# A hybrid diffusion step on one Trainium2 core: more begun strips, two places for a row, two-bank scores, and strips moved into the latents

## The chip, the core and the metric

The kernel runs on one core of one Trainium2 chip. Five engines matter: PE (TensorE, matmuls, with PEld, its weight loads), DVE (VectorE), ACT (ScalarE), POOL (GpSimd) and SP (SyncE, which only issues transfers). The metric is the time of one execution on the device in microseconds; before the change its median over 3 runs is 3182.38 us (3175.32 to 3186.39).

## The reference, cut to what matters

One inference step through two trunk layers, for 128 context tokens and 512 latent ones, 1024 wide. Each layer is half a SwiGLU, a mixer, half a SwiGLU, each behind an RMSNorm with shift, scale and gate from the conditioning.

```python
def swiglu(x, w_gu, w_down):
    g, u = jnp.split(x @ w_gu, 2, axis=-1)
    return (jax.nn.silu(g) * u) @ w_down

def pre(x, g, m, j):
    return rmsnorm(x, g) * (1.0 + m[:, :, 3 * j + 1]) + m[:, :, 3 * j]

# layer 0: p + mu * (0.5 * (prev + next) - p), and conv3(p, w)
# layer 1: latent attention and a long convolution (Hyena), side by side
    s = jnp.einsum('bqhd,bkhd->bhqk', qn, k_nope) + jnp.einsum('bqhr,bkr->bhqk', qp, k_pe)
    prob = jax.nn.softmax(s.astype(jnp.float32) * scale, axis=-1)
    for n, gate in enumerate((x1, x2)):
        z = gate * (bidir_fftconv(z, h[:, n, 0], h[:, n, 1]) + bias[n] * z)
```

`w_gu` is 1024 x 5632, `w_down` 2816 x 1024. Layer 0's mixer projects onto 32 strips of 128 columns (15 for RWKV-7, each shifted as in the comment; 17 for the gated delta rule, 12 of them convolved over three tokens). Layer 1's projects onto 6 strips for the latents of attention (8 heads) and 12 for Hyena.

## The kernel before

All activations lie as [channel, token], in two halves `c` of 320 tokens. Each float32 operand of a large product is split into a rounded part and a rest (`wh`, `wl`, `hh`, `hl`), and a product is three matmuls per 128 channels. The split is a cast on ACT and a subtraction on DVE (L469 to L471, L654, L655). A "strip" is a product with 128 columns of a weight: one load of 512 KB on SP, one cast, one subtraction, 48 matmuls of 320 columns (`strip`, L773).

**A feed-forward block** (`ffn`, L632) has 22 strips of the hidden width in five groups (`FGROUPS`), and after each group a down-projection over 8 column blocks `d`. The 2 x 2 blocks of a strip's gate and up weights against two token halves take seven half products of 12 matmuls (`strip`, L680): the two that need the first half's tokens alone give `u` and `s`, and five need sums and differences of the tokens' quarters (`b`, `hidh`, `hl`, made in `quarters`, L591) and of the weights (`S`, on POOL, L684). The quarters need the norm of the second token half, which comes last out of the branch before. To bridge that, the first `NE` = 5 strips are *begun*: `first` (L666) loads a strip's first weights, makes the two early half products, 24 matmuls, and keeps them in `u2` and `s1` until the strip itself runs, with 60 matmuls then instead of 84. The strip loads the same weights a second time. The four blocks are named by layer and place: 01, 02, 11, 12.

The shift, scale and gate (*modulation*) come from 16 chunks of a 1024 x 1024 product that run in the background of blocks 01 and 02, eight in each. A chunk is four items; an item is four loads of 256 KB into tiles `wmod` and 8 matmuls. `background(n)` (L315) uses n items at a call and `fetch` (L305) loads ahead, `(bufs + 1) // 4` items deep: two, with `NMOD` = 7 tiles. The call stands after each strip and each second `d` (L727, L737).

**Layer 0's input projection** (`in_proj0`, L838) writes each strip as a row `o` of 640 tokens to DRAM (`pd`). The shifted ones (`shift`, L873) sum two neighbours on POOL into `nb` and take one DVE pass; the convolved ones (`conv3`, L906) take two DVE passes. `t` (L275) keeps the first `bufs` with which a name is asked for in a pool; `shift` is called first, and asks for one.

**Layer 1's mixer** (`mixers1`, L2112) runs `latents` (L1635), then four heads of attention with three Hyena strips beside each (`hyena_in`, L1904), then Hyena's transforms (`hyena`, L1934) beside the other four, three parts at each head. A head has a projection and five blocks of 128 queries; a block (L1738) has scores in one or two PSUM banks, a maximum for each bank, an exponential for each with its sum, and joins of both; its weights are transposed on PE and copied to `PT` by DVE (L1779). The last head's output goes to DRAM (`mixd`) and comes back for the output projection.

The program is straight-line code. A scheduler orders each engine's instructions and inserts the waits; each engine, and SP's queue of loads, then runs strictly in that order.

## Time and profile before

| what | value |
|---|---|
| median of 3 runs | 3182.38 us (3175.32 to 3186.39) |
| the profiled execution, its time | 3187.08 us |
| the profiled execution, its span | 3185.1 us |
| granted PE clock, mean | 0.957 |
| block 01, 100 to 564 us: PE busy | 454.64 of 464 us |
| layer 0's mixer, 564 to 1265 us: PE busy | 623.86 of 701 us |
| blocks 02 and 11, 1340 to 2300 us: PE busy | 473.95 of 490 and 446.28 of 470 us |
| layer 1's mixer, 2300 to 2660 us: PE busy | 326.70 of 360 us |
| block 12, 2720 to 3185 us: PE busy | 438.23 of 465 us |

The profile is of one execution. A group row reads: source line, engine, operation, out<-in, shape, count | busy us, mean ns of one | idle us of the engine just before, and what ended it. PE's ends are modelled, so a busy PE is not always a PE at its peak. All matmuls stand on one line (L287), so they are told apart by their operands.

### The profile page before, as it was taken

What the parts mean: (1) busy time and instruction counts of PE and PEld (TensorE: products, weight loads), DVE (VectorE), ACT (ScalarE), POOL (GpSimd) and SP (SyncE); (2) the same over time, 40 slices, a digit from 0 to 9 for tenths busy, and PEclk for the clock granted to TensorE, in tenths of its full rate; (3) what the DMA queues carried; (4) which work ended last, traced back from release to release, by engine and by line L of the source; (5) the groups of instructions that cost most, each with busy time, mean ns of one, the idle gap of its engine ahead of it and who ended that gap; (6) DMA issues with size and microseconds to landing.
All of it is one profiled execution on the core that took longest, in us unless ns stands there. A gap on an engine that the chain in (4) does not pass through costs nothing.

```text
span 3185.1 us, 56006 instructions
## 1 busy us (share of the span) xinstructions
PE 2958.5 (93%) x21505; PEld 2671.5 (84%) x21505; DVE 2267.1 (71%) x4011; ACT 1355.0 (43%) x2846; POOL 1200.8 (38%) x1114
## 2 busy tenths in 40 slices
PE   7799999998988998889999979999989989899998
PEld 2689999987865676879999979999979748899998
DVE  5956667668769666695666797777766786977777
ACT  3423334566365555442333453333545424433333
POOL 1733335225545220263333474444310021744442
PEclk9999999998888989889999989999999989999999
DMA  7465542455564332445553222222321215222222
GB/s 273 137 209 164 177 137 72 166 157 170 139 151 112 93 86 81 161 146 181 163 180 116 82 93 87 84 86 83 122 62 58 91 47 181 67 90 86 80 83 83
DMA packets 277587, 385.36 MB, mean 121 GB/s; under 512 B 128704, under 2 KB 161120, under 8 KB 275400
## 3 DMA queue, kind: packets, MB, share of 16 engines
q1 hardware_dynamic: 277160, 381.13, 38.3%
q8 instruction: 169, 2.77, 0.4%
q14 instruction: 98, 0.80, 0.1%
q0 software_dynamic: 160, 0.66, 0.0%
HBM read 330.29 MB, written 51.42 MB: 120 GB/s over the span
## 4 chain that ended last, share of the span: by engine, by line
PE 54%; DVE 10%; ACT 4%; DMA 4%; POOL 3%; issue 3%; SPq 1%; DVEq 0%; ACTq 0%; POOLq 0%
PE ps L287 52%; DMA wr<-in_wd_dram 2%; DVE wl L655 1%; POOL S L684 1%; DMA wr<-in_wo_dram 1%; DVE nx L539 1%; DVE wl L471 1%; POOL X L826 0%; POOL wl L655 0%; POOL inv L824 0%; PE ps L1778 0%; DMA pd<-o 0%; DVE nacc L514 0%; DVE b L605 0%; ACT wh L470 0%
## 5 line engine op out<-in xcount | busy, mean ns | idle before, releaser
L287 PE MATMUL ps<-hh,wh 128*128 128x320 f32 x2208 | 698.6, 318 | 17.8 <-DVE g L1901 7.1
L287 PE MATMUL ps<-hl,wh 128*128 128x320 f32 x2208 | 695.1, 316 | 5.4 <-POOL hl L546 2.7
L287 PE MATMUL ps<-hh,wl 128*128 128x320 f32 x2208 | 686.5, 315 | 5.3 <-DVE wl L471 4.2
L287 PE MATMUL ps<-b,wh 128*128 128x320 f32 x2112 | 480.5, 315 | 32.5 <-DVE b L605 17.2
L287 PEld LDWEIGHTS ps<-hh,wh 128*128 128x128 f32 x2208 | 422.4, 192 | 34.4 <-DVE g L1901 7.9
L287 PEld LDWEIGHTS ps<-hl,wh 128*128 128x128 f32 x2208 | 422.8, 192 | 9.7 <-POOL hl L546 3.9
L287 PEld LDWEIGHTS ps<-hh,wl 128*128 128x128 f32 x2208 | 420.3, 191 | 8.8 <-DVE wl L471 5.4
L287 PEld LDWEIGHTS ps<-b,wh 128*128 128x128 f32 x2112 | 360.7, 192 | 40.5 <-DVE b L605 19.4
L287 PE MATMUL ps<-hidl,wh 128*128 128x320 f32 x1248 | 383.7, 309 | 0.0
L287 PE MATMUL ps<-hidh,wh 128*128 128x320 f32 x1248 | 383.2, 312 | 0.0
L287 PE MATMUL ps<-hidh,wl 128*128 128x320 f32 x1248 | 381.7, 309 | 1.0 <-DVE wl L471 1.0
L550 DVE SCALAR_TENSOR_TENSOR x<-ps,mod,x 128x128 f32<-128x128 f32 (+2 forms) x528 | 212.4, 435 | 212.3 <-PE ps L287 211.7
L655 POOL TENSOR_TENSOR wl<-S,wh 128x512 fp32r<-128x512 f32 x176 | 260.5, 1480 | 264.8 <-ACT wh L654 261.6
L684 POOL TENSOR_TENSOR S<-wr,wu 128x512 f32<-128x512 f32 x88 | 125.2, 1423 | 600.9 <-DMA wr<-in_wgu_dram 394.9
L287 PE MATMUL ps<-b,wl 128*128 128x320 f32 x1056 | 330.6, 315 | 9.4 <-DVE wl L655 6.1
L470 ACT CAST wh<-wr 128x512 fp32r<-128x512 f32 (+2 forms) x210 | 157.7, 754 | 407.0 <-PE ps L287 318.0
L654 ACT CAST wh<-S 128x512 fp32r<-128x512 f32 (+1 forms) x264 | 201.0, 763 | 216.0 <-PE ps L287 163.7
L471 DVE TENSOR_TENSOR wl<-wr,wh 128x512 fp32r<-128x512 f32 (+2 forms) x210 | 186.5, 891 | 82.9 <-ACT wh L470 80.9
L287 PEld LDWEIGHTS ps<-hidh,wh 128*128 128x128 f32 x1248 | 232.9, 188 | 13.3 <-issue 7.4
L287 PEld LDWEIGHTS ps<-hidh,wl 128*128 128x128 f32 x1248 | 233.4, 188 | 1.5 <-DVE wl L471 1.5
L287 PEld LDWEIGHTS ps<-hidl,wh 128*128 128x128 f32 x1248 | 234.1, 188 | 0.0
L287 PEld LDWEIGHTS ps<-b,wl 128*128 128x128 f32 x1056 | 202.3, 192 | 13.8 <-DVE wl L655 8.5
(457 smaller groups left out, 5971.2 us busy)
## 6 DMA issues: line engine op xcount, KB each, us to landing
wmod<-in_wmod_dram SPq DMA_DIRECT2D x288, 256.0 KB
wr<-in_wgu_dram SPq DMA_DIRECT2D x108, 512.0 KB
wu<-in_wgu_dram SPq DMA_DIRECT2D x88, 512.0 KB
wr<-in_wd_dram SPq DMA_DIRECT2D x80, 320.0 KB
wr<-in_wd_dram SPq DMA_DIRECT2D x96, 256.0 KB
pd<-o SPq DMA_DIRECT2D x32, 320.0 KB
wr<-in_abg_dram SPq DMA_DIRECT2D x17, 512.0 KB
wr<-in_wo_dram SPq DMA_DIRECT2D x16, 512.0 KB
```

Source lines behind the costliest of these rows:

```text
L287: self.nc.tensor.matmul(out=out, lhsT=lhsT, rhs=rhs, start=start, stop=stop)
L470: nc.scalar.copy(out=wh, in_=w)
L471: nc.vector.tensor_sub(out=wl, in0=w, in1=wh.bitcast(F32))
L539: nc.vector.scalar_tensor_tensor(out=xn[:, a:b], in0=self.x[c][:, k, a:b], scalar=A, in1=r[:, a:b], op0=ALU.mult, op1=ALU.mult)
L550: self.nc.vector.scalar_tensor_tensor(out=self.x[c][:, d, a:b], in0=q[:, a:b], scalar=gate[:, cond, d:d + 1], in1=self.x[c][:, d, a:b], op ...
L654: nc.scalar.copy(out=hi, in_=r)
L655: eng.tensor_tensor(out=lo, in0=r, in1=f32(hi), op=ALU.subtract)
L684: G.tensor_tensor(out=out, in0=x, in1=y, op=op)
```

## The change

Five things change.

1. **Begun strips.** `NE` becomes a triple: block 01 keeps 5; block 02, where the second half of the modulation still runs, begins 10; blocks 11 and 12, with no modulation left, begin 9. In block 02 the last six of the ten lie in shared tiles `ew`, and these six take the modulation's weights afterwards: the modulation opens after strip 7, `fetch` is one item deep (six tiles), and 2 items follow each of strips 8 to 16, none stand in the first group's down-projection.
2. **Rows `o`.** Both places are taken at the start, and `shift` uses `conv3` with the weights hmu, omu, hmu; `nb` and POOL's sum go.
3. **Scores.** Both key halves lie in one tile of two PSUM banks: one maximum, one exponential with its sum, no joins.
4. **Strips in the latents.** Three of the twelve Hyena strips run in `latents`: one after the query latents, two at its end. Three heads (`NHS`) take the other nine.
5. **Hyena beside five heads**, two parts at each, and for these heads the copies to `PT` are ACT's.

```diff
-NE = 5
+NE = (5, 10, 9)
...
+NHS = 3
...
+        late = bool(self.bg) and w == 2
+        early, ne = {}, NE[1 if late else 2 if not self.bg else 0]
+        n0 = NE[0] - 1 if late else ne
+        shared = lambda: self.t(fp, [P, 2, H], "ew", bufs=ne - n0)
...
+            if f < n0:
+                p1, s1 = tile("u2", n0), tile("s1", n0 + 1)
+            else:
+                e = shared()
+                p1, s1 = e[:, 0], e[:, 1]
...
-                for f in range(NE):
+                for f in range(ne):
                     first(f)
...
+                if f == (n0 + 3 if late else 1) and self.bg:
+                    if late:
+                        self.open_mod(fp, ne - n0, NCHUNK, lambda: shared().rearrange("p a t -> p (a t)")[:, :D // 2])
+                    else:
+                        self.open_mod(fp, NMOD, NCHUNK)
                     self.fetch()
-                self.background(0 if f < 2 or gi == len(FGROUPS) - 1 else 2 if gi == 0 else 1)
+                if late:
+                    self.background(2 if n0 + 3 < f < FGROUPS[-1][0] else 0)
+                else:
+                    self.background(0 if f < 2 or gi == len(FGROUPS) - 1 else 2 if gi == 0 else 1)
...
-                self.background(d % 2)
+                self.background(0 if late and gi == 0 else d % 2)
...
+        out_ = lambda: self.t(ip, [P, T], "o", bufs=2)
+        for _ in range(2):
+            out_()
...
-            nb = self.t(ip, [P, T + 1], "nb")
-            nc.gpsimd.tensor_tensor(out=nb, in0=p[:, 0:T + 1], in1=p[:, 2:T + 3], op=ALU.add)
-            o = self.t(ip, [P, T], "o")
-            for a, b, g in ((0, LP, 0), (LP, T, 1)):
-                nc.scalar.activation(out=o[:, a:b], in_=p[:, a + 1 + g:b + 1 + g], func=AF.Copy, scale=omu[:, mi:mi + 1])
-                nc.vector.scalar_tensor_tensor(out=o[:, a:b], in0=nb[:, a + g:b + g], scalar=hmu[:, mi:mi + 1],
-                                               in1=o[:, a:b], op0=ALU.mult, op1=ALU.add)
+            o = out_()
+            self.conv3(p, (hmu[:, mi:mi + 1], omu[:, mi:mi + 1], hmu[:, mi:mi + 1]), o)
...
+        next(strips)
...
+        for _ in range(2):
+            next(strips)
...
-            ss = [self.ps("sc") for _ in keys]
-            mx = self.t(ap, [P, 2], "mxs", bufs=4)
-            sm = self.t(ap, [P, 2], "sms", bufs=4)
-            for i, (k0, n) in enumerate(keys):
-                self.mm(ss[i][:, :n], qt[hh][:96, P * qi:P * qi + P], kt[hh][:96, k0:k0 + n])
-                nc.vector.tensor_reduce(out=mx[:, i:i + 1], in_=ss[i][:, :n], axis=mybir.AxisListType.X, op=ALU.max)
-            if len(keys) > 1:
-                nc.vector.tensor_tensor(out=mx[:, :1], in0=mx[:, :1], in1=mx[:, 1:], op=ALU.max)
...
+            sc = self.psum.tile([P, 2, 512], F32, tag="sc", name=self.name("ps"), bufs=2)[:, :len(keys)]
+            n = keys[0][1]
+            mx = self.t(ap, [P, 1], "mxs", bufs=4)
+            sm = self.t(ap, [P, 1], "sms", bufs=4)
+            for i, (k0, _) in enumerate(keys):
+                self.mm(sc[:, i, :n], qt[hh][:96, P * qi:P * qi + P], kt[hh][:96, k0:k0 + n])
+            nc.vector.tensor_reduce(out=mx, in_=sc[:, :, :n], axis=mybir.AxisListType.XY, op=ALU.max)
+            nc.vector.tensor_scalar(out=mx, in0=mx, scalar1=-scale, scalar2=None, op0=ALU.mult)
...
-            for i, (k0, n) in enumerate(keys):
-                nc.scalar.activation(out=pr[:, i * H:i * H + n], in_=ss[i][:, :n], func=AF.Exp, scale=scale, bias=mx[:, :1],
-                                     accum_out=sm[:, i:i + 1])
-            if len(keys) > 1:
-                nc.vector.tensor_tensor(out=sm[:, :1], in0=sm[:, :1], in1=sm[:, 1:], op=ALU.add)
+            nc.scalar.activation(out=pr[:, :nk].rearrange("p (k n) -> p k n", n=n), in_=sc[:, :, :n], func=AF.Exp, scale=scale, bias=mx,
+                                 accum_out=sm)
...
-                nc.vector.tensor_copy(out=PT[hh][:, g:g + n, P * (qi - 1):P * qi],
-                                      in_=q[:, :P * n].rearrange("p (k t) -> p k t", k=n))
+
+                (nc.vector.tensor_copy if hh < NHS else nc.scalar.copy)(out=PT[hh][:, g:g + n, P * (qi - 1):P * qi],
+                                                                        in_=q[:, :P * n].rearrange("p (k t) -> p k t", k=n))
...
-                    q = self.ps("tr")
+                    q = self.ps("tr" if "tr" in self.tags else "mx")
...
-        self.latents(h, first)
+        self.tc.swap_default_side()
+        sp = self.pool("strips", bufs=1, reuse_waits="tile")
+        self.tc.swap_default_side()
+        strips = self.hyena_in(h, sp)
+        self.latents(h, first, strips)
         self.banks(mm=2, sc=4, tr=2)
         ap = self.pool("heads", bufs=1, reuse_waits="tile")
-        sp = self.pool("strips", bufs=1, reuse_waits="tile")
-        heads, strips = self.heads(ap), self.hyena_in(h, sp)
-        for i in range(4):
+        heads = self.heads(ap)
+        for i in range(NHS):
             self.mark(f"head{i}")
             next(heads)
             self.mark("hyin")
             for _ in range(3):
                 next(strips)
...
-        for i in range(4, 8):
+        for i in range(NHS, 8):
             self.mark(f"head{i}")
             next(heads)
             self.mark("hyena")
-            for _ in range(3):
+            for _ in range(2):
                 next(conv, None)
```

How the order changes at three places. The first is DVE at the start of block 12, from the first split of a quarter on; `wl<-wr` is the subtraction of a begun strip, `s` its sum, `wl<-S` that of the first whole strip, and `b`, `hidh`, `hl` are the quarters. Before:

```order
L605 TENSOR_TENSOR b_5205_29057<-hidh_5200_29052,b_5204_29056 128x1280
L655 TENSOR_TENSOR wl_29274<-S_5256_29261,wh_29273 128x1024
L617 TENSOR_TENSOR hidh_5202_29054<-hidl_5203_29055,hidh_5202_29054 128x1280
L616 TENSOR_TENSOR hidh_5200_29052<-hidl_5203_29055,hidh_5200_29052 128x1280
L673 TENSOR_TENSOR s_5247_29236<-ps_29238,u_5246_29235 128x320
L605 TENSOR_TENSOR b_5207_29059<-hidh_5200_29052,b_5206_29058 128x1280
L605 TENSOR_TENSOR b_5209_29061<-hidh_5202_29054,b_5208_29060 128x1280
L605 TENSOR_TENSOR hl_29070<-hidl_5203_29055,hh_29069 128x1280
L605 TENSOR_TENSOR hl_29070<-hidl_5201_29053,hh_29069 128x1280
```

After:

```order
L607 TENSOR_TENSOR b_5163_28911<-hidh_5158_28906,b_5162_28910 128x1280
L657 TENSOR_TENSOR wl_29145<-wr_29142,wh_29144 128x1024
L619 TENSOR_TENSOR hidh_5160_28908<-hidl_5161_28909,hidh_5160_28908 128x1280
L683 TENSOR_TENSOR s_5205_29090<-ps_29092,u_5204_29089 128x320
L618 TENSOR_TENSOR hidh_5158_28906<-hidl_5161_28909,hidh_5158_28906 128x1280
L657 TENSOR_TENSOR wl_29181<-wr_29178,wh_29180 128x1024
L683 TENSOR_TENSOR s_5212_29126<-ps_29128,u_5211_29125 128x320
L657 TENSOR_TENSOR wl_29217<-wr_29214,wh_29216 128x1024
L607 TENSOR_TENSOR b_5165_28913<-hidh_5158_28906,b_5164_28912 128x1280
L607 TENSOR_TENSOR b_5167_28915<-hidh_5160_28908,b_5166_28914 128x1280
L607 TENSOR_TENSOR hl_28924<-hidl_5161_28909,hh_28923 128x1280
L683 TENSOR_TENSOR s_5219_29162<-ps_29164,u_5218_29161 128x320
```

Three subtractions of begun strips and one more of their sums stand now between the first `b` and the first `hl`, and the first whole strip's subtraction has moved behind them.

The second is PE in the latents of layer 1, around the sum of squares of the query latents (`acc,const`); `wvh,ch` is the value projection. Before:

```order
L287 MATMUL ps_25562<-hh_25210,wl_25557 128x320
L287 MATMUL ps_25562<-hh_25210,wh_25556 128x320
L287 MATMUL ps_25562<-hl_25211,wh_25556 128x320
L287 MATMUL ps_25562<-hh_25210,wl_25557 128x320
L287 MATMUL ps_25617<-acc_25432,const_58 128x320
L287 MATMUL ps_25618<-acc_25432,const_58 128x320
L287 MATMUL ps_25641<-wvh_25635,ch_25363 128x512
L287 MATMUL ps_25641<-wvh_25635,cl_25364 128x512
```

After:

```order
L288 MATMUL ps_25664<-hh_25224,wl_25659 128x320
L288 MATMUL ps_25664<-hh_25224,wh_25658 128x320
L288 MATMUL ps_25634<-acc_25449,const_58 128x320
L288 MATMUL ps_25635<-acc_25449,const_58 128x320
L288 MATMUL ps_25664<-hl_25225,wh_25658 128x320
L288 MATMUL ps_25664<-hh_25224,wl_25659 128x320
L288 MATMUL ps_25664<-hh_25224,wh_25658 128x320
L288 MATMUL ps_25664<-hl_25225,wh_25658 128x320
L288 MATMUL ps_25664<-hh_25224,wl_25659 128x320
L288 MATMUL ps_25794<-hh_25013,wh_25789 128x320
L288 MATMUL ps_25794<-hl_25014,wh_25789 128x320
L288 MATMUL ps_25794<-hh_25013,wl_25790 128x320
```

The first moved Hyena strip (into `ps_25664`) is spread around the two `acc` matmuls, and a second one (into `ps_25794`) follows where the value projection stood.

The third is PE in block 02 where the fourth group's down-projection ends; `cond` with `wmod` or `ew` is the modulation, two matmuls to a row. Before, the last item stands alone:

```order
L287 MATMUL ps_19036<-hidl_3259_18269,wh_19016 128x320
L287 MATMUL ps_19036<-hidh_3258_18268,wl_19017 128x320
L287 MATMUL ps_18729<-wmod_18894,cond_15447 32x256 x2
L287 MATMUL ps_18729<-wmod_18896,cond_15447 32x256 x2
L287 MATMUL ps_18729<-wmod_18898,cond_15447 32x256 x2
L287 MATMUL ps_18729<-wmod_18900,cond_15447 32x256 x2
L287 MATMUL ps_19066<-hidh_3256_18266,wh_19061 128x320
L287 MATMUL ps_19066<-hidl_3257_18267,wh_19061 128x320
```

After:

```order
L288 MATMUL ps_19150<-hidh_3202_18122,wh_19130 128x320
L288 MATMUL ps_19150<-hidl_3203_18123,wh_19130 128x320
L288 MATMUL ps_19150<-hidh_3202_18122,wl_19131 128x320
L288 MATMUL ps_19077<-ew_19086,cond_16591 32x256 x2
L288 MATMUL ps_19077<-ew_19088,cond_16591 32x256 x2
L288 MATMUL ps_19077<-ew_19090,cond_16591 32x256 x2
L288 MATMUL ps_19077<-ew_19092,cond_16591 32x256 x2
L288 MATMUL ps_19077<-ew_19172,cond_16591 32x256 x2
L288 MATMUL ps_19077<-ew_19174,cond_16591 32x256 x2
L288 MATMUL ps_19077<-ew_19176,cond_16591 32x256 x2
L288 MATMUL ps_19077<-ew_19178,cond_16591 32x256 x2
L288 MATMUL ps_19077<-ew_19188,cond_16591 32x256 x2
```

The last three items now stand in one row of 24 matmuls, with six tiles to load them into.

More of the change, by code (lines that the diff above doesn't have):

```diff
@@ L391, in close_x, with open_mod @@
         self.close(self.np, self.xp)
-    def open_mod(self, pool, bufs, chunks):
+    def open_mod(self, pool, bufs, chunks, tile=None):
         self.mp, self.mbufs, self.steps = pool, bufs, chunks * KD // 2
+        self.mtile = tile or (lambda: self.t(pool, [P, D // 2], "wmod", bufs=bufs))
         self.cond = self.t(pool, [P, KD, 32], "cond")
@@ L413, in go @@
                     for c in range(0, D, 2 * W):
-                        w = self.t(self.mp, [P, 2 * W], "wmod", bufs=self.mbufs)
+                        w = self.mtile()
                         nc.sync.dma_start(out=w, in_=self.I["wmod"][l, j, kk, :, c:c + 2 * W])
@@ L690, in strip @@
             else:
-                u, g0 = tile("u2", NE), tile("s1", NE + 1)
+                u, g0 = tile("u2", n0), tile("s1", n0 + 1)
                 a11, a12 = parts((g, V))
@@ L723, in ffn @@
                 strip(f, B, lambda c, s: self.split(hid[c][0][:, f - fa], hid[c][1][:, f - fa], s))
-                if f == 1 and self.bg:
-                    self.open_mod(fp, NMOD, NCHUNK)
+                if f == (n0 + 3 if late else 1) and self.bg:
[3 more added lines that the diff above has]
+                        self.open_mod(fp, NMOD, NCHUNK)
                     self.fetch()
-                self.background(0 if f < 2 or gi == len(FGROUPS) - 1 else 2 if gi == 0 else 1)
+                if late:
+                    self.background(2 if n0 + 3 < f < FGROUPS[-1][0] else 0)
+                else:
+                    self.background(0 if f < 2 or gi == len(FGROUPS) - 1 else 2 if gi == 0 else 1)
             if gi == len(FGROUPS) - 1:
@@ L852, in gate @@
             q = self.strip(I["abg"][0], h)
-            o = self.t(ip, [P, T], "o", bufs=2)
+            o = out_()
             for c in range(2):
@@ L860, in conv @@
             q = self.strip(I["abg"][1 + i], h)
-            o = self.t(ip, [P, T], "o", bufs=2)
+            o = out_()
             if j == 3:
@@ L876, in shift @@
             self.padded(q, p)
[L877 to L883 removed]
+            o = out_()
+            self.conv3(p, (hmu[:, mi:mi + 1], omu[:, mi:mi + 1], hmu[:, mi:mi + 1]), o)
             if func is not None:
@@ L1633, in small_split, with latents @@
         return out
-    def latents(self, h, first):
+    def latents(self, h, first, strips):
         nc, I = self.nc, self.I
@@ L1740, in softmax @@
             nk = sum(n for _, n in keys)
[L1741 to L1757 removed]
+            sc = self.psum.tile([P, 2, 512], F32, tag="sc", name=self.name("ps"), bufs=2)[:, :len(keys)]
[6 more added lines that the diff above has]
+            nc.vector.tensor_scalar(out=mx, in0=mx, scalar1=-scale, scalar2=None, op0=ALU.mult)
+            pr = S[hh, qi] = self.t(ap, [P, 2 * H], "pr", bufs=2)
+            nc.scalar.activation(out=pr[:, :nk].rearrange("p (k n) -> p k n", n=n), in_=sc[:, :, :n], func=AF.Exp, scale=scale, bias=mx,
+                                 accum_out=sm)
+            nc.vector.reciprocal(out=sm, in_=sm)
+            nc.vector.tensor_scalar(out=pr[:, :nk], in0=pr[:, :nk], scalar1=sm, scalar2=None, op0=ALU.mult)
         def values(hh, qi):
@@ L2128, in mixers1 @@
         next(strips, None)
+        self.tc.swap_default_side()
         self.close(sp)
+        self.tc.swap_default_side()
         self.close_w()
```

5 lines of the change are left out of this document (removed).

## The prediction

> **What bounds the kernel now.** I read the page first, then the table by stage, then for each stage that the change touches the waits and the costs.
>
> ```profile
> PE 2958.5 (93%) x21505; PEld 2671.5 (84%) x21505; DVE 2267.1 (71%) x4011; ACT 1355.0 (43%) x2846; POOL 1200.8 (38%) x1114
> ```
>
> TensorE (PE) is busy for 93% of the span of 3185.1 us. The change removes no matmul, so all that it can win is the idle 226.6 us, and of these only what lies in the stages that it touches. The table by stage shows where that is (start:end, length, then the busy time of PE, PEld, DVE, ACT and POOL with their counts, the granted clock, DMA share, GB/s):
>
> ```profile
> 564.00:905.00 341.00, 301.11 (x2172) 283.84 (x2170) 224.80 (x381) 188.72 (x380) 145.44 (x241) 0.91 0.53 155
> 1340.00:1440.00 100.00, 85.26 (x584) 77.92 (x583) 86.43 (x96) 42.91 (x72) 61.14 (x36) 0.91 0.43 144
> 1840.00:1930.00 90.00, 67.96 (x407) 63.73 (x408) 85.76 (x88) 42.61 (x74) 69.27 (x39) 0.89 0.26 89
> 2300.00:2380.00 80.00, 67.44 (x369) 61.79 (x368) 54.38 (x70) 36.40 (x67) 15.24 (x11) 0.91 0.29 92
> 2380.00:2525.00 145.00, 144.96 (x925) 130.52 (x926) 99.84 (x254) 71.21 (x196) 10.17 (x8) 1.00 0.16 49
> 2525.00:2660.00 135.00, 114.31 (x433) 67.18 (x431) 110.43 (x247) 32.62 (x97) 28.53 (x20) 0.93 0.27 91
> 2725.00:2805.00 80.00, 66.89 (x401) 62.58 (x400) 77.78 (x80) 36.43 (x60) 61.05 (x33) 0.94 0.22 75
> ```
>
> From the top: layer 0's input projection (PE idle 39.9 us), the starts of three feed-forward blocks (14.7, 22.0 and 13.1 us idle, with DVE at 86 to 97%), the latents of layer 1 (12.6 us idle), four heads beside twelve strips (PE never idle), and four heads beside Hyena (20.7 us idle, DVE at 82%). When nothing is late, PE sets the pace. From the chain of waits, in order of time (start, length, matmuls):
>
> ```profile
> 1926.06 330.41 PE ps L287 x2252
> ```
>
> That is 0.1467 us for a matmul of 320 columns, and 7.04 us for a strip of 48.
>
> **A. The mixer of layer 1 (2300 to 2660).** Three of the twelve strips go into the latents, and the fourth head goes from the strips to Hyena. The latents' waits, by line (the last column is PE's idle time before the group and what ended it):
>
> ```profile
> L287 PE MATMUL ps<-qh,wh 128*128 128x320 f32 x12 | 4.7, 392 | 2.1 <-ACT k L1725 2.0
> L287 PE MATMUL ps<-acc,const 128*128 128x320 f32 x4 | 2.5, 781 | 3.7 <-POOL acc L1660 3.7
> L287 PE MATMUL ps<-ch,wh 128*128 128x384 f32 x4 | 1.4, 362 | 1.0 <-ACT wh L475 1.0
> ```
>
> Three strips bring 21.1 us of matmuls and fifteen transposes of 128 columns (an estimated 0.06 us each by their width, 0.9). They stand in front of these 6.8 us of waits, which they can cover (their loads go out among the latents' own, at a DMA share of 0.29); the other 5.8 us of the stage's idle time come before them. So the latents grow by 22.0 - 6.8 = 15.2 us (9.4 if all 12.6 us are covered, 22.0 if none). The heads' section loses one head and three strips of four times as many, a quarter of 145: -36.25 us, since PE bounds it throughout.
>
> That head lands beside Hyena. On PE it costs at most (144.96 - 12 x 7.04) / 4 = 15.1 us, so the section has 114.31 + 15.1 = 129.4 us of PE work. Whether it still fits into 135 us hangs on DVE, which the change relieves. Over both sections the DVE groups concerned are:
>
> ```profile
> L1746 DVE TENSOR_REDUCE mxs<-ps 128x1 f32<-128x320 f32 x64 | 30.2, 484 | 3.9 <-PE ps L287 3.6
> L1779 DVE COPY PT<-ps 128x512 f32<-128x512 f32 x32 | 21.9, 686 | 8.9 <-PE ps L1778 8.8
> L1779 DVE COPY PT<-ps 128x128 f32<-128x128 f32 x32 | 9.1, 284 | 2.5 <-PE ps L1778 2.5
> L1755 DVE TENSOR_TENSOR sms<-sms 128x1 f32<-128x1 f32 x32 | 8.7, 273 | 9.8 <-ACT pr L1752 9.4
> L1748 DVE TENSOR_TENSOR mxs<-mxs 128x1 f32<-128x1 f32 x32 | 7.6, 239 | 0.2
> L1746 DVE TENSOR_REDUCE mxs<-ps 128x1 f32<-128x128 f32 x8 | 2.3, 286 | 1.7 <-PE ps L287 1.7
> ```
>
> From 128 to 320 elements a maximum grows by 198 ns, so one over 640 should take 484 + 330 = 0.81 us; with the two small joins gone, a block of queries saves 0.97 - 0.81 + 0.27 + 0.24 = 0.67 us, a head 2.7. The copies of the transposed weights, 4 x 0.97 = 3.9 us a head, go to ACT, which is busy 32.62 of 135 us. Five heads save 33 us of DVE and the new one costs (99.84 - 12 x 3.5) / 4 = 14.5, where 3.5 us is an estimate of a strip's own DVE work, one subtraction (1.23, the row of `kl` below) and four convolution passes (2 x 0.589 + 2 x 0.562, rows of part B): 110.43 + 14.5 - 33 = 92 us. DVE is then no bound. The one maximum now waits for both score matmuls; behind it on DVE stands only work of the block before, so I cost that at nothing, and at half a microsecond a block (20 blocks, 10 us) if DVE were still full. What PE waits for it there now is
>
> ```profile
> L287 PE MATMUL ps<-div,yy 128*128 128x256 f32 x64 | 16.1, 402 | 5.6 <-DVE t L1735 5.6
> L287 PE MATMUL ps<-y,dfp 128*128 128x512 f32 x4 | 3.7, 1090 | 5.1 <-DVE t L1735 5.1
> L471 DVE TENSOR_TENSOR kl<-wr,kh 128x1024 fp32r<-128x1024 f32 x1 | 1.2, 1226 | 7.4 <-DMA mixd<-om 7.4
> ```
>
> where the third row is the end of the section: the last head's output goes through DRAM before the output projection can start, and that stays. With about 5.6 us of waits left the section ends as long as it was: 0 (-5.6 with no wait left, +15.1 if the head covers nothing). A is 15.2 - 36.25 + 0 = **-21.0 us**, with ends of -32 and +1.
>
> **B. The input projection of layer 0.** Before, all rows `o` share one place, since the first call that names it asks for one. ACT and the chain show it:
>
> ```profile
> ACT o L911 <- DMA pd<-o: 35.1, 9, 11.9
> ACT o L881 <- DMA pd<-o: 22.4, 9, 6.0
> 739.80 5.13 DMA pd<-o
> 836.02 4.53 DMA pd<-o
> 895.96 2.42 DMA pd<-o
> ```
>
> Two places take these 12.1 us off the chain. Next late there are SyncE's runs of issues and ACT's own chain, so I count half. The fifteen shifts swap POOL's sum and one DVE pass for two DVE passes:
>
> ```profile
> L882 DVE SCALAR_TENSOR_TENSOR o<-nb,hmu,o 128x128 f32<-128x128 f32 (+1 forms) x30 | 18.3, 631 | 9.8 <-ACT o L881 7.4 <-POOL nb L878 2.3
> L912 DVE SCALAR_TENSOR_TENSOR o<-pp,cols,o 128x128 f32<-128x128 f32 (+1 forms) x24 | 13.9, 589 | 33.0 <-ACT o L911 32.9
> L913 DVE SCALAR_TENSOR_TENSOR o<-pp,cols,o 128x128 f32<-128x128 f32 (+1 forms) x24 | 13.2, 562 | 0.4
> ```
>
> So DVE gains 15 x 2 x (0.589 + 0.562 - 0.631) = 15.6 us in a stage where it is busy for 66%: hidden, mostly. B is **-6 us** (ends -12 and 15.6 - 12.1 = +3.5).
>
> **C. The begun strips.** Each further one moves 24 matmuls, 3.52 us, ahead of the quarters' splits, and one load of 512 KB, one cast, one 1024-column subtraction and one sum with them. The loads are extra, since the strip itself loads the same weights again: one in 3.52 us, behind SyncE's earlier loads, at a DMA share of 0.22 in that stretch; I cost them at nothing. In the last block PE and DVE show:
>
> ```profile
> L287 PE MATMUL ps<-b,wh 128*128 128x320 f32 x120 | 30.4, 343 | 8.4 <-DVE b L605 5.4 <-ACT b L604 3.0
> L605 DVE TENSOR_TENSOR hl<-hidl,hh 128x1280 fp32r<-128x1280 f32 x2 | 6.7, 3364 | 0.0
> L605 DVE TENSOR_TENSOR b<-hidh,b 128x1280 fp32r<-128x1280 f32 x3 | 6.3, 2142 | 0.9 <-ACT b L604 0.9
> L655 DVE TENSOR_TENSOR wl<-wr,wh 128x1024 fp32r<-128x1024 f32 x2 | 5.0, 2514 | 0.4 <-ACT wh L654 0.4
> L673 DVE TENSOR_TENSOR s<-ps,u 128x320 f32<-128x320 f32 x5 | 2.4, 471 | 0.3 <-PE ps L287 0.3
> 2743.02 1.48 DVE L605 TENSOR_TENSOR b<-hidh,b 128x1280 fp32r<-128x1280 f32 x1
> ```
>
> The four extra strips put up to 4 x (2.51 + 0.47) = 11.9 us on DVE, which has no slack there. But the same splits take 1.48 us when POOL is quiet, so 2 x 1.88 + 3 x 0.66 = 5.7 us of DVE's stretch is POOL's doing, and in the new order POOL's sums for the first whole strip stand behind the begun strips' loads. I take +3 us for the stretch; its ends are 4 x (1.23 + 0.47) - 5.7 = +1, with POOL quiet, and +12. The return comes later, in strips 5 to 8, which then need 60 matmuls (8.8 us) and not 84 (12.3). What such a strip takes is shown by the last SiLU of each strip, in the block's first four strips (begun ones) and in three of its second group (whole ones):
>
> ```profile
> L709 ACT ACTIVATE u<-u x4: 472/473/474, 2767.0 to 2800.4; 128x320 f32<-128x320 f32 x4
> L709 ACT ACTIVATE u<-u x3: 472/473/474, 2854.9 to 2879.6; 128x320 f32<-128x320 f32 x3
> L476 DVE TENSOR_TENSOR hidl<-nsq,hidh 128x320 fp32r<-128x320 f32 x3 | 4.7, 1579 | 0.0
> L476 DVE TENSOR_TENSOR hidl<-nsq,hidh 128x320 fp32r<-128x320 f32 x4 | 1.9, 481 | 0.0
> ```
>
> 33.4 / 3 = 11.1 us for a begun strip, 24.7 / 2 = 12.35 for a whole one. The begun ones do not reach PE's 8.8, because DVE and POOL hold each other up: the same subtraction takes 1579 ns among them (third row) and 481 among whole strips (fourth). The Trainium skill (SBUF — State Buffer, section "Who interferes with whom") states it as a rule: a VectorE instruction with two SBUF inputs and a GpSimd one that reads SBUF shut each other out, and the later one waits for the whole of the other. The trace agrees; by that rule alone the returned strips keep the pace of 11.1.
>
> So four strips return between 4 x 1.25 = 5.0 and 4 x 3.52 = 14.1 us; the down-projection between groups gives DVE and POOL some room, and I take the middle, 9.5. A block with nine begun strips wins 6.5 us, at most its 13.1 us of idle time; there are two: -13. The block with ten returns 11.9 for five strips and pays 3.7. Its modulation weights now wait until strip 7, six tiles and one item deep where it was seven and two. Six items that stood among begun strips and so cost little now stand in PE's busy part: at 8 matmuls of PE's pace, an estimated 1.2 us each, less four that fall beside strips 8 and 9, +2.4. For waits on their loads I add 3 (see the second rival). That block wins 3. C is **-16 us** (ends -40, the idle time of the three blocks, and +28, with three stretches at their upper end and strips returned at the lower).
>
> **The sum** is -21 - 6 - 16 = -43 us. The profiled execution took 3187.1 us, 4.7 above the median of 3182.4; taken off the median, 3139.4 us. The Trainium skill (TensorE: Matmul & The Clock Gate, section "What's actually happening") says that an idle window of about 3.4 us halves the array's clock until it has been busy as long; the table agrees in kind (clock 0.91 in the latents, 1.00 beside the strips). By it, removed waits would bring some us more; my sum leaves that out.
>
> **The rivals.** First, DVE and POOL hold every returned strip at 11.1 us and the extra subtractions cost their full price, so that C is nothing: -27, 3155.4 us. For it speaks that DVE has 2 us of slack in 80; against it that POOL's sums move away. Chance 0.19. Second, and slower than before: the modulation weights of the second feed-forward block, one item deep, make PE wait at each of the 31 items behind the first.
>
> ```profile
> PE ps L287 <- DMA wmod<-in_wmod_dram: 10.6, 4, 4.0
> ```
>
> At the mean of these four waits, 2.65 us, that is 82 us, and -43 - 3 + 82 = +36 gives 3218 us. It decides from (43 + 3) / 31 = 1.5 us an item on. Against it: the new order puts some 40 other matmuls ahead of the second half of most items that follow another. Chance 0.06. Third, Hyena's own chain of products and not DVE's load sets the pace there, and the fifth head comes on top whole: A is -6, the sum -28, 3154 us. Against it: the waits named above are for DVE's `t`, a small step of a head behind a queue. Chance 0.13. Fourth, the change does not fill what it aims at: strips, shifts and begun strips only move waits on, all terms end near zero, about -5, 3177 us. Chance 0.07. My forecast has 0.55.
>
> **The numbers.** All best ends together give -84 us, all worst +32. Leaving out about one chance in ten on each side I take -72 to -10: 3110 to 3172 us. What a measurement of this kernel can tell from no change is about 0.3%, 9.5 us. Faster by more is the forecast and the first and third rival, less their upper edges: 0.85; within it 0.08; slower 0.07.
>
> **What would show it.** A is right if the section from the latents to the output projection is some 20 us shorter than 360, PE's idle time beside Hyena is under 10 us and DVE's share there is below 75%. B is right if no `o` waits for `pd<-o` and the chain no longer runs through it. C is right if PE waits for `b` less than 3 us in each of the three blocks and strips 5 to 8 follow each other at under 10.5 us; at 11.1 the first rival holds. PE waits on the modulation weights of over 40 us would make the second rival true. A time above 3172 us makes the prediction wrong; so does one inside the range with A and C in the wrong proportion.

## The result and the profile after

The changed kernel takes 3160.43 us (median of 4 runs, 3156.41 to 3163.04), the kernel before 3183.58 (4 runs): a ratio of 0.993, 95% interval 0.9909 to 0.9952, so about 23 us less, a little over half of the 43 that were forecast. The profiled executions took 3187.08 us before (above its median) and 3156.41 after (the fastest of the four), 30.7 apart; the stage lengths below go by these two.

The page of the changed kernel, first the span, then the busy times:

```profile
span 3154.6 us, 55911 instructions
PE 2949.8 (94%) x21505; PEld 2657.8 (84%) x21505; DVE 2225.0 (71%) x3905; ACT 1364.0 (43%) x2823; POOL 1172.8 (37%) x1099
```

PE ran the same 21505 matmuls; its idle time went from 226.6 to 204.8 us. The ends of the stages can be read to a tenth of a microsecond from writes that both kernels make: the last row `o`, each residual sum into `x`, Hyena's first matmul on `zt`.

| stage | before, us | after, us | difference | forecast |
|---|---|---|---|---|
| block 01 | to 581.5 | to 582.0 | +0.4 | 0 |
| input projection of layer 0, to the last `o` | 317.7 | 296.5 | -21.2 | -6 (B) |
| chunks and output projection of layer 0 | 448.9 | 456.1 | +7.2 | none |
| block 02 | 495.6 | 505.4 | +9.8 | -3 (C) |
| block 11 | 456.3 | 450.3 | -6.1 | -6.5 (C) |
| latents, to the first score | 79.9 | 94.9 | +15.0 | +15.2 (A) |
| heads beside strips | 146.4 | 111.8 | -34.6 | -36.25 (A) |
| heads beside Hyena, to the output projection | 134.7 | 141.5 | +6.8 | 0 (A) |
| output projection and block 12 | 512.4 | 504.4 | -8.0 | -6.5 (C) |

The same stretches in the table by stage of the changed kernel (columns as in the prediction):

```profile
564.00:884.00 320.00, 288.52 (x2173) 273.46 (x2171) 232.38 (x412) 188.41 (x381) 123.75 (x223) 0.96 0.53 159
...
1334.50:1839.90 505.40, 487.00 (x3445) 447.83 (x3444) 344.41 (x530) 185.54 (x322) 216.55 (x146) 0.99 0.46 147
...
2290.00:2385.00 95.00, 86.78 (x528) 82.09 (x527) 62.55 (x84) 47.23 (x90) 15.10 (x11) 0.96 0.29 95
2385.00:2496.00 111.00, 110.86 (x703) 100.42 (x703) 70.87 (x158) 52.46 (x128) 7.20 (x7) 1.00 0.16 52
...
2496.90:2638.40 141.50, 122.29 (x491) 72.90 (x489) 101.29 (x192) 47.67 (x119) 32.71 (x22) 0.97 0.25 85
```

The latents idle 8.2 us instead of 12.6, the heads beside strips never. Three rows are worse than the forecast. The chunks behind layer 0's input projection take 7.2 us more. Block 02 (1334.5 to 1839.9) is longer although it lost its waits; and beside Hyena PE idles 19.2 us, where under 10 was expected, with DVE busy for 72% of the section. Block 02 before, as one row, says where to look:

```profile
1348.20:1843.80 495.60, 476.42 (x3446) 446.74 (x3444) 349.92 (x530) 187.68 (x322) 216.46 (x149) 0.98 0.46 147
```

PE's idle time there is about the same, 19.2 us before and 18.4 after. The waits behind it changed hands; of before, then of after:

```profile
PE ps L287 <- DVE b L605: 7.8, 2, 5.5
PE ps L287 <- ACT b L604: 4.6, 2, 4.1
```

```profile
PE ps L288 <- POOL wl L657: 6.8, 3, 5.4
PE ps L288 <- DMA ew<-in_wmod_dram: 4.0, 1, 4.0
PE ps L288 <- DVE wl L657: 3.4, 5, 1.0
```

The begun strips took the 12.4 us for the quarters `b` away, and brought 10.2 for the splits of a strip's own weights (`wl`; 0.2 before). So it is PE's *busy* time that grew, by 10.6 us for the same number of matmuls, at a granted clock of 0.98 before and 0.99 after. The group of the modulation's matmuls in that block, before and then after, shows most of it:

```profile
L287 PE MATMUL ps<-wmod,cond 128*32 128x256 f32 x512 | 36.1, 385 | 2.3 <-DMA wmod<-in_wmod_dram 2.3
```

```profile
L288 PE MATMUL ps<-ew,cond 128*32 128x256 f32 x512 | 44.7, 393 | 4.0 <-DMA ew<-in_wmod_dram 4.0
```

The timeline of PE in the changed kernel (start, length, count; an item is 8 matmuls, and each stands as two records) shows why one record lasts about as long and the 512 together longer:

```profile
1499.28 1.07 PE L288 MATMUL ps<-ew,cond 128*32 128x256 f32 x16
...
1504.73 0.63 PE L288 MATMUL ps<-ew,cond 128*32 128x256 f32 x4
...
1505.77 0.63 PE L288 MATMUL ps<-ew,cond 128*32 128x256 f32 x4
...
1506.97 0.63 PE L288 MATMUL ps<-ew,cond 128*32 128x256 f32 x4
...
1730.90 3.74 PE L288 MATMUL ps<-ew,cond 128*32 128x256 f32 x24 [4.00 <-DMA ew<-in_wmod_dram]
```

An item (16 records) in one go takes 1.07 us. With tiles for only one item and a half, the order takes part of the items up one weight tile at a time, in pieces of four records and 0.63 us: 2.5 us for a whole item. Of the 512 records 100 stand in 25 such pieces, where the kernel before has three. Counted from the start of the matmul ahead of each row to the start of the one behind it, less the 0.147 us of one matmul, the modulation costs PE 50.0 us in this block, and cost 38.9 before. At the end of the background work PE waits 4.0 us for a transfer, and the last 24 records then come at the pace of the six tiles that land (3.74 us).

The waits of PE in the starts of blocks 11 and 12, after:

```profile
PE ps L288 <- DVE nacc L508: 7.7, 1, 7.7
PE ps L288 <- DVE wl L657: 4.8, 4, 2.3
PE ps L288 <- POOL wl L657: 3.4, 2, 3.0
```

```profile
PE ps L288 <- DVE hl L607: 3.1, 1, 3.1
PE ps L288 <- POOL wl L657: 2.8, 2, 2.1
PE ps L288 <- DVE wl L657: 1.8, 3, 0.8
```

No wait for `b` is left here either; the wait for `nacc` stood there before, with the same 7.7 us. The last SiLU of strips 5 to 8 of block 12:

```profile
L719 ACT ACTIVATE u<-u x4: 466/472/473, 2833.8 to 2861.4; 128x320 f32<-128x320 f32 x4
```

27.6 / 3 = 9.2 us a strip: not 11.1, as the first rival had it, and nearly PE's 8.8.

### The profile page after: what moved, and what is told of

Its sections match the earlier page's. It is cut to its first block, busy times and chain, and to the rows that moved or that the text cites. A ratio compares the mean times of both kernels' runs of the same rounds, so it can differ in the third digit from the quotient of the medians.

```text
span 3154.6 us, 55911 instructions
## 1 busy us (share of the span) xinstructions
PE 2949.8 (94%) x21505; PEld 2657.8 (84%) x21505; DVE 2225.0 (71%) x3905; ACT 1364.0 (43%) x2823; POOL 1172.8 (37%) x1099
## 4 chain that ended last, share of the span: by engine, by line
PE 48%; DVE 9%; DMA 3%; issue 2%; ACT 2%; POOL 0%; SPq 0%; DVEq 0%; ACTq 0%; POOLq 0%
PE ps L288 47%; DVE wl L657 2%; DMA wr<-in_wd_dram 1%; DVE hidl L478 1%; DMA wr<-in_wo_dram 1%; DVE wl L473 0%; DVE nx L541 0%; PE ps L1793 0%; DVE nx L720 0%; ACT wh L656 0%; DVE nacc L516 0%; DVE u L697 0%; DVE nsq L697 0%; DMA wr<-in_wgu_dram 0%; DVE nacc L508 0%
## 5 line engine op out<-in xcount | busy, mean ns | idle before, releaser
L288 PE MATMUL ps<-hh,wh 128*128 128x320 f32 x2208 | 693.7, 316 | 15.2 <-DVE g L1917 7.1
L288 PE MATMUL ps<-b,wh 128*128 128x320 f32 x2112 | 470.3, 312 | 3.8 <-DVE b L607 3.2
L288 PEld LDWEIGHTS ps<-hh,wl 128*128 128x128 f32 x2208 | 417.9, 190 | 13.5 <-DVE wl L657 6.6
L288 PEld LDWEIGHTS ps<-hidh,wh 128*128 128x128 f32 x1248 | 232.8, 188 | 12.8 <-issue 7.0
```

The costliest lines, as they stand in the source:

```text
L288: self.nc.tensor.matmul(out=out, lhsT=lhsT, rhs=rhs, start=start, stop=stop)
```

## The experiments

Twelve kernels, in three groups (1 to 4; 5, 6, 7 and 10; 8, 9, 11 and 12), each group with the kernel before on the same chip: 3177.0, 3173.1 and 3176.5 us (medians of seven). Seven of the twelve ran once, and a single time says little, so most are read by the length of the one stage that they touch.

**1. Block 02 as before.** Five begun strips there, the modulation behind strip 1.

```diff
-NE = (5, 10, 9)
+NE = (5, 5, 9)
-        late = bool(self.bg) and w == 2
+        late = False
```

> Undone in the feed-forward block that begins at 1334.5 us of the changed kernel's trace: it begins five strips again and takes the modulation's weights from its own seven tiles behind strip 1. All else stays changed. In the changed kernel this block took 505.4 us against 495.6 before. Theory (the moved modulation costs more than the begun strips return): the block falls back to 494 to 498 us, the modulation's matmuls from 46.1 to about 34 us of PE, and the median falls from 3160 to about 3151. Rival (something ahead of the block, not its own edit, slows it, such as the weights that it finds loaded): the block stays at 502 us or more and the median within 3157 to 3164.

```profile
1339.10:1835.00 495.90, 477.74 (x3445) 448.30 (x3443) 349.50 (x529) 187.81 (x322) 216.30 (x146) 0.98 0.44 147
```

```profile
L288 PE MATMUL ps<-wmod,cond 128*32 128x256 f32 x512 | 36.3, 386 | 2.0 <-DMA wmod<-in_wmod_dram 2.0
```

The block is back at 495.9 us and the matmuls at 36.3 (the expectation counted from start to start, hence 34). The median is 3144.51 us, ratio 0.9907 (0.9888 to 0.9927). So it is the block's own edit that costs 9.5 us: in the eight traces with the changed code here the block takes 503.9 to 506.4 us. Which part of the edit it is, the next kernel tells.

**2. Two items deep.** Ten begun strips and the late modulation stay; two more tiles are shared.

```diff
-        n0 = NE[0] - 1 if late else ne
+        n0 = NE[0] - 3 if late else ne
-                if f == (n0 + 3 if late else 1) and self.bg:
+                if f == (n0 + 5 if late else 1) and self.bg:
-                    self.background(2 if n0 + 3 < f < FGROUPS[-1][0] else 0)
+                    self.background(2 if n0 + 5 < f < FGROUPS[-1][0] else 0)
```

> Same block, ten begun strips kept, modulation still begun behind strip 7, but eight shared tiles in place of six (two whole items of four weight tiles deep in place of one and a half; two of the begun strips stand in plain tiles in place of four). Theory (one item deep: items are taken up in pieces of a tile or two and the last ones wait for their transfer): most of the 12.3 us that the modulation's matmuls grew by goes, they take 35 to 39 us, and the block takes 494 to 499 us. Rival (later items cost as much however deep, since two now stand beside each strip, or the begun strips themselves cost it): the block stays at 502 to 506 us.

```profile
1330.60:1823.30 492.70, 475.99 (x3446) 448.03 (x3444) 343.08 (x530) 185.39 (x322) 216.76 (x146) 0.99 0.45 151
```

```profile
L288 PE MATMUL ps<-ew,cond 128*32 128x256 f32 x512 | 35.5, 386 | 2.5 <-DMA ew<-in_wmod_dram 2.5
```

492.7 us, a little better than expected; the matmuls fall from 44.7 to 35.5 us with everything else in place. The median is 3143.69 us, ratio 0.990 (0.9884 to 0.9917). The rival, that late items or begun strips cost it, falls: the depth costs it. The pieces of four are down to three again, and two items stand in one row of 32 records. Kernels 10 and 11 below, with the same depth, give 492.3 and 491.4 us. The waits for `wl` stay (6.8 and 3.0 us); so even with the depth mended, ten begun strips give this block 2.9 to 4.2 us.

**3 and 4. The two halves of part 2.** Two places and the old shift (its sum on POOL in two pieces); then one place and the new shift.

```diff
-            self.conv3(p, (hmu[:, mi:mi + 1], omu[:, mi:mi + 1], hmu[:, mi:mi + 1]), o)
+            for a, b, g in ((0, LP, 0), (LP, T, 1)):
+                nb = self.t(ip, [P, T - LP], "nb")[:, :b - a]
+                nc.gpsimd.tensor_tensor(out=nb, in0=p[:, a + g:b + g], in1=p[:, a + g + 2:b + g + 2], op=ALU.add)
...
```

> Layer 0's input projection with two places for its out rows, as changed, but the shift computed as before: a sum of two neighbours on POOL, in two pieces of 128 and 512 columns, then the two scaled terms. In the changed kernel the last out row is written at 877 us, before at 894. Theory (the wait for the one place is what was saved): the last out row still comes at 875 to 880 us and no out row waits for the transfer of another. Rival (the hand-over from POOL to DVE inside each shift is what was saved): it comes at 888 us or later.

```diff
-        out_ = lambda: self.t(ip, [P, T], "o", bufs=2)
-        for _ in range(2):
-            out_()
+        out_ = lambda: self.t(ip, [P, T], "o", bufs=1)
```

> The mirror of the run before: one place for the out rows, and the shift without POOL's sum. Theory (the wait for the place): the out rows wait for their transfers again, some 2 to 5 us each, and the last out row comes at 888 to 896 us. Rival (the hand-over): it comes at 875 to 880 us. Half and half would put both runs at about 885.

What the engines waited for in front of their work on `o`, in the kernel before, with places only, and with the new shift only (us in all, times):

```profile
  DMA pd<-o: 65.6, 22
```

```profile
  DMA pd<-o: 12.0, 5
```

```profile
  DMA pd<-o: 57.0, 18
```

The last `o` came at 876.1 us with the places only and at 897.8 with the shift only (878.4 changed, 899.3 before). (The expectations counted the last convolved row, which starts its last pass at 893.9 us in kernel 4 and at 894.5 before.) In the length of the stage all of the 21 us are the places'; the shift is worth nothing either way. The single times were 3145.67 and 3168.63 us.

**5 and 6. Where Hyena runs.** Four heads beside it in place of five; then three parts at each head in place of two.

```diff
-NHS = 3
+NHS = 4
...
-            for _ in range(3):
+            for _ in range(3 if i == 0 else 2):
                 next(strips)
```

> One head fewer beside Hyena: four heads with the nine remaining strips (three, two, two, two), then four heads beside Hyena with two parts each; all else as changed. From Hyena's first matmul to the last head's output the changed kernel takes 138 to 142 us (five heads), the kernel before 131 (four heads, single-bank scores); the heads beside the strips take 111.8 us. A head is worth about 13.5 us of PE (67.7 us of the heads' matmuls in the section over five). Theory (Hyena's own chain, mostly its products on DVE, sets the section, and a head beside it costs only what it takes from DVE in those stretches): with one head fewer the section takes 130 to 135 us, the strips' section 123 to 127, and layer 1's mixer is 4 to 9 us longer. Rival (the fifth head costs its whole PE time wherever it stands): the section takes 125 to 128 us and the mixer is as long as before within 2 us.

With one head fewer the heads are done 113.3 us after Hyena's first matmul, but the output projection starts at 133.6. The rows are the time to the last head's output and the rest:

```profile
2509.50:2622.80 113.30, 100.56 (x369) 55.85 (x368) 82.19 (x162) 36.99 (x94) 27.14 (x19) 0.94 0.21 70
2622.80:2643.10 20.30, 12.32 (x58) 10.08 (x57) 4.88 (x11) 2.58 (x5) 0.00 (x0) 0.88 0.68 231
```

The mark that both theories named, the last head, was badly chosen: here Hyena ends the section. Its last result (`x`) stands at 127.1 us; PE then waits 7.3 us, for the output projection's weights, whose load is issued behind Hyena's last store. Read to the output projection the section takes 133.6 us against 141.5 (141.5 to 145.4 in the six runs with the change's code in the mixer), and the strips' section 125.3 against 111.8. The whole mixer takes 353.9 us; the seven runs so far with the mixer as changed, or with only its order changed, gave 348.2 to 353.7, 351.5 in the mean. So with the head taken back the mixer is some 2 us longer and not 4 to 9, and this run settles neither side. A fifth head beside Hyena costs 8 to 12 us read to the output projection, and 11 to 15 read to the last result of either kind, of its 13.5 us of PE.

```diff
-            for _ in range(2):
+            for _ in range(3):
                 next(conv, None)
```

> Hyena's six parts go out three beside each head, as before the change, instead of two; five heads as changed. The order in which work is offered then puts Hyena's chain ahead of the heads. Theory (the chain of Hyena's products is what the section ends on, so offering it earlier shortens it): Hyena's first matmul to the last head's output falls from 138 to 142 us to 131 to 136. Rival (the heads have then nothing to fill PE with at the end, or the order is set by what is ready anyway): 138 us or more.

142.6 us: the theory fails, the order of offering does not matter. It does move Hyena: its last result now stands at 115.5 us, where the six runs above have 131.8 to 133.0, and the section is no shorter. So Hyena's chain by itself does not set the section with five heads. (Single times 3162.95 and 3161.09 us.)

**7 to 9. DVE's load beside Hyena**, one instruction group at a time: the scaling of `pr` off DVE, the copies to `PT` onto it, and the single-bank scores of the kernel before.

```diff
-            nc.vector.tensor_scalar(out=pr[:, :nk], in0=pr[:, :nk], scalar1=sm, scalar2=None, op0=ALU.mult)
+            if hh < NHS:
+                nc.vector.tensor_scalar(out=pr[:, :nk], in0=pr[:, :nk], scalar1=sm, scalar2=None, op0=ALU.mult)
+            else:
+                nc.scalar.activation(out=pr[:, :nk], in_=pr[:, :nk], func=AF.Copy, scale=sm)
```

> For the five heads beside Hyena the scaling of the probabilities (18 of 128 x 640 at 856 ns and 4 smaller on DVE, 17.1 us in the section) runs on ACT, which is busy 47.7 of 141.5 us there. Theory (DVE, full in Hyena's two product stretches of some 25 us each, sets the section): Hyena's first matmul to the last head's output falls by 3 to 8 us, to 132 to 137. Rival (PE's own work and the chain through it set the section; DVE's load is only beside it): it stays at 138 to 142, or rises, since ACT stands in the chain of each head.

```diff
-                (nc.vector.tensor_copy if hh < NHS else nc.scalar.copy)(out=PT[hh][:, g:g + n, P * (qi - 1):P * qi],
+                nc.vector.tensor_copy(out=PT[hh][:, g:g + n, P * (qi - 1):P * qi],
```

> The transposed probabilities of the five heads beside Hyena are copied by DVE again, as for the first three heads (19 of 128 x 512 and 19 of 128 x 128, 16.2 us on ACT in the section); all else as changed. Theory (DVE sets the section beside Hyena): about 15 us more on DVE lengthen it from 138 to 142 us to 145 to 155. Rival (DVE has room outside Hyena's products: 101 of 141 us busy): 139 to 144.

For the third, `softmax` stands as in the kernel before (the removed lines of the change put back).

> The scores in single banks again, with two maxima, two exponentials and their joins; all else as changed. Theory (DVE sets the section beside Hyena, PE the section beside the strips, where it was busy 111.7 of 111.8 us): the strips' section stays at 111 to 114 us, the section beside Hyena grows from 138 to 142 to 144 to 152. Rival (the joins sit in the chain of every head and hold PE everywhere): the strips' section grows by 4 us or more too; or the other way, both stay as they are and part 3 was worth nothing.

The section, from Hyena's first matmul to the output projection, with the scaling on ACT:

```profile
2495.50:2632.40 136.90, 123.40 (x495) 72.68 (x493) 87.88 (x170) 62.71 (x142) 31.42 (x22) 0.98 0.26 89
```

with the copies on DVE:

```profile
2495.10:2647.10 152.00, 127.31 (x496) 74.36 (x494) 114.86 (x235) 33.49 (x80) 32.40 (x22) 0.95 0.23 80
```

with the old scores, first the heads beside strips:

```profile
2388.20:2499.20 111.00, 111.00 (x704) 100.66 (x705) 75.52 (x200) 55.74 (x156) 8.13 (x7) 1.00 0.17 54
2499.20:2654.50 155.30, 133.59 (x496) 77.65 (x494) 110.78 (x249) 51.63 (x155) 31.00 (x22) 0.91 0.23 78
```

To the last head's output these are 133.3, 148.4 and 151.8 us against 137.9 to 142.0 with the code of the change: all three inside what the theory named. 13 us of DVE less give 5 to 9 us; 14 more cost 6 to 11. These two also shift as much work onto ACT or off it, but the section moves the way of DVE's load, not of ACT's. The old scores cost 10 to 14 for 9.5 us of DVE, so there DVE's load is not all of it; what the rest is was not tried. The scores in two banks are worth nothing beside the strips (111.0 and 111.8) and 10 to 14 us beside Hyena. Single times: 3150.84, 3163.19, 3173.06 us.

**10 to 12. Put together.** Kernel 2 with the old shift of kernel 3:

> The changed kernel with both earlier edits: eight shared tiles in the feed-forward block with the moved modulation (alone: 3143.7 us against 3160 of the changed kernel), and the shift with its sum on POOL (alone: the last out row as early as in the changed kernel, but the time from it to the end of layer 0's output projection 442.3 us against 456.1). Theory (the shift without POOL costs DVE time that the work after it, on the same DVE, pays): that stretch is again 440 to 446 us and the median 3126 to 3136. Rival (that stretch varies from run to run by as much: it was 457.6 and 452.7 us in the two other runs with the same code there): 450 to 458 us, and the median 3140 to 3146.

The rival holds: 3144.86 us, ratio 0.9904 (0.9886 to 0.9922), and 454.7 us from the last `o` to the end of the output projection. Kernel 3's 442.3 did not repeat; its granted clock there was 0.92 where the other eleven kernels with two places had 0.87 to 0.89; why is open:

```profile
876.10:1318.40 442.30, 386.37 (x4381) 298.16 (x4380) 313.77 (x836) 248.23 (x757) 125.16 (x256) 0.92 0.43 121
```

Kernel 2 with the scaling on ACT of kernel 7 (its diff above):

> The changed kernel with eight shared tiles (two whole items of the modulation deep) and the probabilities of the five heads beside Hyena scaled on ACT. Alone the first took 12.7 us off its block (505.4 to 492.7), the second 4 to 8 us off the section beside Hyena (138 to 142, to 133.3). Theory (the two stand in stages that do not touch): they add, and the median is 3134 to 3142, ratio to before 0.986 to 0.990. Rival (a stage ahead gives its gain back in the next, as layer 0's chunks did): 3143 or more.

3139.59 us (3135.47 to 3143.49), ratio 0.9886 (0.9861 to 0.991). By the stages the two add (block 02 491.4 us, beside Hyena 136.9); the ratios of this kernel and of kernel 2 cannot be told apart, since their intervals overlap.

And on top of it, an item at each of the eight steps of the last down-projection that has any:

```diff
-                self.background(0 if late and gi == 0 else d % 2)
+                self.background(0 if late and gi == 0 else 1 if late and gi == len(FGROUPS) - 2 else d % 2)
```

> The kernel of the run before, and in the last down projection ahead of the modulation's end an item at each of the eight steps, in place of each second one, so that no item is left to be taken up in a row at its end (with eight tiles three items stood there, 7.8 us of PE for 48 matmuls against 1.0 for 16 elsewhere, 2.5 of it a wait for a transfer). Theory (those items wait for their transfers one after the other): the stretch of that projection and what follows falls from 112.5 to 105 to 108 us, the median 4 to 7 us below the run before. Rival (the transfers are late at each step then, since two tiles of four items cannot come in within a step): 110 us or more.

3139.58 us, ratio 0.9882 (0.986 to 0.9903). The stretch did fall, from 112.3 to 103.6 us, but the group ahead of it, where the items now stand, rose from 91.2 to 98.3. The block takes 490.5 us in place of 491.4: the time only moved, which neither theory had named.

## Why the prediction was right and where it was not

The sign and the range held; of the 43 us named, 23 came (31 in the pair of profiles). The three terms missed by +8, -8 and +11 us, so "A and C in the wrong proportion" applies: by its own sign the prediction's account of A and C is wrong, though the time lies in the range. That B gave 8 us more than forecast and made up for part of the rest is luck. The measured 3160.4 us lies nearer to the first and third rivals (3155.4 and 3154) than to the forecast's 3139.4.

**A, -21.0 forecast, -12.8 measured to the start of the output projection** (-8 to -13 over the six runs with this code). The latents (+15.0 for +15.2) and the strips' section (-34.6 for -36.25) came as worked out. The step that failed is "110.43 + 14.5 - 33 = 92 us. DVE is then no bound". DVE was busy for 101.3 us, and it was a bound.

The mis-sized term is the 33. Kernels 8 and 9 put its two parts back one at a time: DVE's busy time rises by 13.6 us with the copies (forecast 5 x 3.9 = 19.5) and by 9.5 with the old scores (5 x 2.7 = 13.5), 23.1 in all. With 23.1 in its place the sum gives 101.8. The 33 was added up from the durations of rows, and these overlap: in the section before, the durations of all DVE instructions add up to 128.2 us, within 111.0 us of busy time. The maximum over 640 took what was estimated (0.82 us for 0.81).

A duration also depends on the neighbours. In the changed kernel the scaling of `pr` and the maximum, first beside the strips and then beside Hyena:

```profile
L1766 DVE TENSOR_REDUCE mxs<-ps 128x1 f32<-128x640 f32 x15 | 12.3, 823 | 3.2 <-PE ps L288 3.1
L1772 DVE TENSOR_SCALAR pr<-pr,sms 128x640 f32<-128x640 f32 x14 | 7.7, 552 | 0.5
...
L1772 DVE TENSOR_SCALAR pr<-pr,sms 128x640 f32<-128x640 f32 x18 | 15.4, 856 | 0.7
L1766 DVE TENSOR_REDUCE mxs<-ps 128x1 f32<-128x640 f32 x17 | 13.9, 818 | 3.1 <-PE ps L288 3.0
```

The same scaling takes 552 ns where POOL is busy 7 of 111 us and 856 where it adds Hyena's products, 5.5 us over 18 of them. One by one, the ten that no POOL instruction overlaps take 540 to 554 ns, and seven of the eight that one overlaps 948 to 1604. The maximum, which reads PSUM, does not change. The Trainium skill (SBUF — State Buffer, section "Who interferes with whom") has both: a `tensor_scalar` can run in a mode in which it and GpSimd shut each other out, and on trn2 a `tensor_reduce` never contends. The trace agrees.

Nor is the share of the section what counts. In two stretches, Hyena's products, DVE is full:

```profile
2523.00:2549.00 26.00, 20.83 (x66) 10.33 (x66) 25.64 (x48) 7.75 (x20) 11.46 (x8) 1.00 0.22 69
2575.00:2600.00 25.00, 20.82 (x79) 12.24 (x77) 24.15 (x43) 7.45 (x19) 6.81 (x5) 1.00 0.15 42
```

Kernels 7 and 8 show that DVE's load moves the section in both directions. PE's longest waits before the output projection, 3.4 and 3.2 us for a head's `t`, end at 2599.1 and 2603.1 us, at the end of the second stretch; with the scaling off DVE (kernel 7) the waits for `t` fall from 6.6 to 0.7 us in all. So the third rival (Hyena's chain sets the pace, the fifth head on top whole) had a price near what came, 8 to 12 us for 15, and the wrong cause: kernel 6 ends Hyena early and gains nothing. The prediction's argument against it, that the waits were for a small step behind a queue, was true, but the queue was DVE's own.

**B, -6 forecast, -14 measured.** The mechanism was right and the size was off. Its first sign did not hold whole: engines still waited for `pd<-o` (5 times, 15.4 us, for 22 and 65.6). Its second cannot be read, since the chain of the changed kernel's trace begins behind this stage. But the input projection fell by 21. The mis-sized term is "so I count half" of the 12.1 us on the chain: more than the chain's own sum went. Of this the chunks gave back some 6 us (446 and 449 us with one place, 453 to 460 in eleven of twelve runs with two); what holds them back there was not tried. That the shift would be hidden was right.

**C, -16 forecast, -5.4 measured** (+9.8, -6.1 and -9.1 without the output projection). Both of its signs held, no wait for `b` and strips 5 to 8 at 9.2 us, and the first rival's 11.1 falls. But neither sign tests the modulation in block 02. What failed there is "an estimated 1.2 us each" for a moved item with "3 for waits on their loads": an item taken up a tile at a time costs 2.5, and the pieces and the slow last tiles cost 9.2 us of PE's busy time (44.7 against 35.5 in kernel 2). The second rival, one item deep, had the right place, a price of 82 us that was far too high, and the wrong form: in PE's idle time only the last wait shows, 4.0 us.

Blocks 11 and 12 came near the forecast by two errors that offset, which is luck. Up to the first residual sum they are longer by 8.3 us (94.8 to 103.1) and 4.5 us (91.1 to 95.6), where +3 was taken. The group of strips 5 to 8 is shorter by 12.2 us (54.1 to 41.9) and 11.0 us (54.0 to 43.0) and the rest of the block by 1.9 and 2.7: the four strips return 14.1 and 13.7 us, nearly the upper end of 4 x 3.52 = 14.1, where the middle, 9.5, was taken. So it is with the 2.9 us of block 02 in kernel 2, the forecast's own 3: the way to its first residual sum is 8.4 us longer there (92.8 to 101.2), and 3.7 was forecast.

One end of the range was also added up wrongly. The best end of C, -40, is called the idle time of the three blocks, but the table gives 14.7 + 22.0 + 13.1 = 49.8 us. The forecast does not depend on it.

## What to carry to other kernels

Background work has a price that depends on how it is taken up: keep its prefetch at whole items, two at least, before moving it to where the main engine is full. Do not subtract a sum of instruction durations from an engine's busy time: durations overlap, and they depend on the neighbours (552 or 856 ns here). And before calling an engine free at 72%, look for stretches in which it is full: one in a chain can set the stage.

## What was not expected of the hardware

Splitting an item's run of 16 records into four pieces costs PE 2.5 us in place of 1.07, without an idle row in the waits: the loss stands in the busy time. By the starts, in the run of 16 four records start within 20 ns and the next four 0.22 to 0.24 us later; in a piece of four two start within 10 ns and the other two 0.24 us later. So four records take two steps in place of one, and each piece has its own way in and out: the matmul behind starts 0.55 us after the first of four records, and 1.00 us after the first of sixteen. A weight tile holds two of an item's four column blocks, which may be why only two start together; no kernel here tests that. And the stretch behind layer 0's input projection, with one and the same code, took 452.7 to 459.5 us over ten runs, a wider spread than block 11 (449.5 to 451.3): a single run says little about it.
